# 320 unused bytes ahead of the experts' activations in SBUF

## The chip, the cores and the metric

The kernel runs on one NeuronCore of a Trainium2 chip. The metric is the device time of one execution in microseconds (us). The median of three runs of the kernel before is 1845.49 us (1844.25 to 1846.53). The profile comes from a further execution, which took 1848.51 us, 1846.7 us of it between the first and the last instruction.

## The reference

One layer: a gated short convolution, then a mixture of 16 SwiGLU experts in which each expert chooses its 256 tokens out of 2048. The model width and the experts' inner width are both 1024, and everything is float32.

```python
hl = modulate(rms_norm(lat, norm_g[i, 0]), sh1, sc1)
gate_b, gate_c, v = jnp.split(hl @ w_in, 3, axis=-1)
lat = lat + g1 * ((gate_b * dwconv_centred(gate_c * v, conv_w)) @ w_out)
hl2 = modulate(rms_norm(lat, norm_g[i, 1]), sh2, sc2)
lat = lat + g2 * expert_choice_ffn(hl2, router, w_gate, w_up, w_down)

def expert_choice_ffn(h, w_router, w_gate, w_up, w_down):
    cap = EC_CAPACITY_FACTOR * N // N_EXPERTS            # 256
    aff = jax.nn.softmax((h @ w_router).astype(jnp.float32), axis=-1)
    g, idx = lax.top_k(jnp.swapaxes(aff, 1, 2), cap)
    xs = jax.vmap(lambda hb, ib: hb[ib])(h, idx)
    hid = silu(einsum('becd,edf->becf', xs, w_gate)) * einsum('becd,edf->becf', xs, w_up)
    ys = einsum('becf,efd->becd', hid, w_down) * g[..., None]
    return zeros.at[idx].add(ys)                         # by token
```

## The kernel before

Every large product is made of three matmuls in the type float32r, on a high part and a low part of each operand: high times high, high times low, low times high. ScalarE (ACT) copies a float32 tile into its high part, and VectorE (DVE) subtracts that from the original to get the low part. Such a group of three is called a triple below.

**The mixer stages.** The input projection (L514, L515, L517), its recombined form (L875 to L877) and the output projection (L1133, L1134, L1136) multiply tiles from the pool `mix` with split weights `ws` from the pool `weights`, or two tiles of `mix` with each other. Their matmuls stream 512 columns.

**The experts.** A piece of weights (512 KB) is loaded by SyncE's queue into `raw`, split into one of eight buffers `ws`, and used from there. `gate_up(e, fh)` makes one half of an expert's inner activations. Its stationary operand is a 128x128 block of `ws`, its moving operand 256 columns of the gathered tokens `xT` (L1604, L1606, L1608), 192 matmuls in all. Then SiLU and the product go through `sg`, and the split result lands in `hT`, of which there are four buffers (L1614 to L1619). `down(e, dh)` multiplies the other way round: the stationary operand is a 128x128 block of `hT`, the moving operand 512 columns of `ws` (L1671 to L1673). It makes 48 matmuls, 16 triples, and the scaled result goes to `ot` (L1690), from which GpSimd's queue scatters it into the output. The second half of the last expert (`last_down`) makes 8 triples of that kind and then 48 matmuls of 256 columns (L1660 to L1662).

The order of the work is written out by hand: for expert e from 2 on, `gate_up(e, 0)`, `down(e-1, 0)`, `gate_up(e, 1)`, `down(e-1, 1)`. `pick` (L1534), which makes the list of an expert's tokens with 16 small bf16 matmuls, stands inside `down(e-1, 0)`, ahead of its third k. For the third expert, it stands inside `gate_up(1, 1)`.

**Where tiles lie.** A pool lays its tiles one behind the other in each partition, in the order in which their tags are first asked for. In the pool `moe`, that order is `raw`, `ax`, `oh`, `xs`, `xT`, `hT`, `sg`, `ot`. The byte address of a tile within its partition, modulo 512, is called its remainder here. All offsets that a matmul adds inside these tiles are multiples of 512 bytes, so an operand has the remainder of its tile. In the built program:

| tile | first address | remainder before | remainder of the change |
|---|---|---|---|
| `ws`, eight buffers (weights) | 44928 | 384 | 384 |
| matmul operands of the mixer (`hl`, `sb`, `tg`) | 130432 | 384 | 384 |
| `xT`, two buffers | 147008 | 64 | 64 |
| `hT`, four buffers | 179776 | 64 | 384 |
| `sg`, two buffers | 212544 | 64 | 384 |
| `ot`, three buffers | 216640 | 64 | 384 |

The other tiles of the pool stand ahead of `hT` and keep their addresses.

Of the kernel before, what the change touches and what calls it, by code (L numbers as in the profile page):

```python
# [7 lines left out]
F32 = mybir.dt.float32  # L8
# [9 lines left out]
P = 128  # L18
# [28 lines left out]
def block_kernel(ctx: ExitStack, tc, x, c, ada_w, ada_b, norm_g, w_in, conv, w_out, router, wg, wu, wd, out):  # L47
# [188 lines left out]
    def split_high(i):  # L236
        nonlocal n_high
        while n_high <= min(i, len(pieces) - 1):
            load_to(n_high)
            t = wpool.tile([P, 2] + pieces[n_high][3], F32R, name="ws", tag="ws", bufs=n_split)  # L240
            nc.scalar.activation(t[:, 0], raws[n_high], AF.Copy)  # L241
            ws_of[n_high] = t
            n_high += 1

    def split_low(i, eng=None, part=0, n=1):
        nonlocal n_done
        split_high(i)
        t, raw = ws_of[i], raws[i]
        w = pieces[i][3][-1] // n
        s = slice(part * w, (part + 1) * w)  # L250
        (eng or nc.vector).tensor_sub(t[:, 1, ..., s], raw[..., s], t[:, 0, ..., s].bitcast(F32))  # L251
        if part == n - 1:
            raws.pop(i)
            if i in extra:
                extra.remove(i)
            n_done += 1
            load_to(i + depth())
# [1255 lines left out]
    moe = ctx.enter_context(tc.tile_pool(name="moe", bufs=1, reuse_waits="tile"))  # L1513
# [72 lines left out]
    def gate_up(e, fh, between=lambda k: None):  # L1586
        xT = xT_of[e]
        if fh == 0:
            hT_of[e] = {}
        ps = [[mm.tile([P, 2, CAP], F32, name="pm", tag="mm") for _ in range(2)] for _ in range(2)]  # L1590
        for kk in range(KD // 2):
            for j in range(2):
                k = 2 * kk + j
                n = w_moe[0, e, fh, kk] + n_split - 2 + j
                split_high(n)
                between(k)
                while n_done <= min(n, len(pieces) - 1):
                    split_low(n_done)
                for f in range(4):
                    c0 = slice(f * P, (f + 1) * P)  # L1600
                    for m in range(2):
                        o = ps[m][f // 2][:, f % 2]
                        w = ws_of[w_moe[m, e, fh, kk]]
                        nc.tensor.matmul(o, w[:, 0, j, c0], xT[:, 0, k], start=(k == 0 and f % 2 == 0), stop=False,  # L1604
                                         skip_group_check=True)
                        nc.tensor.matmul(o, w[:, 0, j, c0], xT[:, 1, k], start=False, stop=False,  # L1606
                                         skip_group_check=True)
                        nc.tensor.matmul(o, w[:, 1, j, c0], xT[:, 0, k], start=False, stop=(k == KD - 1),  # L1608
                                         skip_group_check=True)
        hT = moe.tile([P, 2, 4, CAP], F32R, name="hT", tag="hT", bufs=4)  # L1610
        hT_of[e][fh] = hT
        sgs = [moe.tile([P, 2, CAP], F32, name="sg", tag="sg", bufs=2) for _ in range(2)]
        for f2, sg in enumerate(sgs):
            nc.scalar.activation(sg, ps[0][f2], AF.Silu)  # L1614
            nc.vector.tensor_mul(sg, sg, ps[1][f2])
        for f2, sg in enumerate(sgs):
            t = slice(2 * f2, 2 * f2 + 2)
            nc.scalar.activation(hT[:, 0, t], sg, AF.Copy)
            nc.vector.tensor_sub(hT[:, 1, t], sg, hT[:, 0, t].bitcast(F32))  # L1619
# [114 lines left out]
    for e in range(E):  # L1734
        if e == 0:
            gate_up(0, 0, lambda k: pick_oh(1) if k == 1 else pick(1) if k == 3 else
                    (tick(k), turn(1, 0) if k == 7 else None) if k in (2, 4, 5, 6, 7) else None)
            gate_up(0, 1, lambda k: join(1, k // 2 - 2) if k in (4, 6) else
                    turn(1, 1) if k == 1 else tick(k) if k in (0, 2, 3, 5) else None)
            continue  # L1740
        if e == 1:
            gate_up(1, 0, lambda k: tick(k) if k not in (0, 2) else None)
            down(0, 0, tick)
            for _ in rounds:
                pass
            pick_oh(2)
            gate_up(1, 1, lambda k: pick(2) if k == 1 else turn(2, k - 4) if k in (4, 5) else
                    join(2, 0) if k == 7 else None)
        else:
            if e + 1 < E:  # L1750
                pick_oh(e + 1)
            gate_up(e, 0)
            down(e - 1, 0, (lambda kk: pick(e + 1) if kk == 1 else None) if e + 1 < E else (lambda kk: None))
            gate_up(e, 1, (lambda k: turn(e + 1, k // 2 - 1) if k in (2, 4) else join(e + 1, 0) if k == 7 else None)
                    if e + 1 < E else (lambda k: None))
        down(e - 1, 1, (lambda kk: join(e + 1, 1) if kk == 1 else None) if e + 1 < E else (lambda kk: None))
# [24 lines left out]
```

## Time and profile before

| what | value |
|---|---|
| runs, us | 1845.49, 1844.25, 1846.53 |
| profiled execution, us | 1848.51 |
| its span, us | 1846.7 |
| mean granted TensorE clock | 0.988 |
| VectorE, ScalarE, GpSimd busy | 69%, 50%, 17% |
| the experts' matmuls, first to last start | 766.5 to 1836.9 us |

Starts and durations are of one profiled execution. The recorded duration of a matmul (276 ns with 256 columns, about 390 ns with 512) is longer than the time from its start to the next one's, since matmuls overlap in the array. The time that a stream of matmuls takes is therefore read from the distance of their starts, not from their durations. A start is given to 0.01 us by the timeline, so a distance is taken over many matmuls.

### The profile page before, as it was taken

To read this page: it belongs to the slowest core of one execution; us is meant where nothing else is said; L and a number is where in the kernel's file an instruction comes from. 1 tells how busy PE (TensorE), PEld (TensorE's weight loads), DVE (VectorE), ACT (ScalarE), POOL (GpSimd) and SP (SyncE) were. 2 spreads that over 40 slices of the span, in tenths; PEclk is the share of its full clock that TensorE was granted. 3 is DMA by queue.
4 is the path that set the end of the run, shared out by engine and by line. 5 is a ranking of instruction groups with operands and counts; after the bars stand their busy time and mean duration, and the time that the engine had idled before them with its cause. 6 is when DMAs were issued, how large, how long until landed. Compare 5 with 4: busy or idle time off the path is not lost.

```text
span 1846.7 us, 29333 instructions
## 1 busy us (share of the span) xinstructions
PE 1791.2 (97%) x11415; PEld 1594.1 (86%) x11415; DVE 1281.7 (69%) x1840; ACT 919.6 (50%) x1244; POOL 320.2 (17%) x466
## 2 busy tenths in 40 slices
PE   7999999999999997699999999999999999999997
PEld 6787888788888885698899999999999999999996
DVE  6787878888766678786765666666576566666653
ACT  4665454333345555474554455455455445545541
POOL 2324101111111223200210210211121021021002
PEclk9999999999999998799999999999999999999999
DMA  9756566555578994677687787877978878787774
GB/s 338 238 178 205 168 224 192 169 170 152 169 241 258 242 258 153 204 224 206 216 240 242 250 231 230 256 224 236 256 223 244 240 250 232 230 257 226 233 223 80
DMA packets 309771, 406.78 MB, mean 220 GB/s; under 512 B 103284, under 2 KB 174240, under 8 KB 309632
## 3 DMA queue, kind: packets, MB, share of 16 engines
q1 hardware_dynamic: 283632, 312.59, 55.7%
q0 software_dynamic: 26000, 92.33, 16.8%
q8 instruction: 89, 1.46, 0.3%
q14 instruction: 50, 0.41, 0.1%
HBM read 318.34 MB, written 63.98 MB: 207 GB/s over the span
## 4 chain that ended last, share of the span: by engine, by line
PE 88%; DVE 5%; DMA 2%; ACT 2%; issue 1%; POOL 0%; SPq 0%; POOLq 0%; DVEq 0%; ACTq 0%
PE pm L1604 12%; PE pm L1606 12%; PE pm L1608 12%; PE pm L876 7%; PE pm L877 7%; PE pm L875 7%; PE pm L1673 6%; PE pm L1671 6%; PE pm L1672 6%; PE pm L1133 2%; PE pm L1134 2%; PE pm L1136 2%; PE pm L514 1%; PE pm L515 1%; PE pm L517 1%
## 5 line engine op out<-in xcount | busy, mean ns | idle before, releaser
L251 DVE TENSOR_TENSOR ws<-raw,ws 128x1024 fp32r<-128x1024 f32 x390 | 463.8, 1222 | 272.9 <-ACT ws L241 272.9
L241 ACT ACTIVATE ws<-raw 128x1024 fp32r<-128x1024 f32 x390 | 394.5, 1053 | 408.8 <-PE pm L1608 325.2
L1604 PE MATMUL pm<-xT,ws 128*128 128x256 f32 x2048 | 568.6, 278 | 1.1 <-ACT xT L1583 1.1
L1606 PE MATMUL pm<-xT,ws 128*128 128x256 f32 x2048 | 567.3, 277 | 1.9 <-DVE xT L1584 1.8
L1608 PE MATMUL pm<-xT,ws 128*128 128x256 f32 x2048 | 566.9, 277 | 0.0
L1606 PEld LDWEIGHTS pm<-xT,ws 128*128 128x128 f32 x2048 | 385.9, 188 | 3.9 <-DVE xT L1584 2.1
L1604 PEld LDWEIGHTS pm<-xT,ws 128*128 128x128 f32 x2048 | 385.2, 188 | 2.7 <-ACT xT L1583 1.5
L1608 PEld LDWEIGHTS pm<-xT,ws 128*128 128x128 f32 x2048 | 385.2, 188 | 0.0
L1701 POOL DMA_INDIRECT out_dram<-ot,idx x30 | 105.0, 3498 | 587.9 <-DVE ot L1690 583.9
L1673 PE MATMUL pm<-ws,hT 128*128 128x512 f32 x504 | 198.4, 394 | 0.0
L1671 PE MATMUL pm<-ws,hT 128*128 128x512 f32 x504 | 198.3, 393 | 0.0
L1672 PE MATMUL pm<-ws,hT 128*128 128x512 f32 x504 | 197.1, 391 | 0.0
L875 PE MATMUL pm<-tg,sb 128*128 128x512 f32 x472 | 185.8, 394 | 0.0
L877 PE MATMUL pm<-tg,sb 128*128 128x512 f32 x472 | 183.8, 389 | 0.0
L876 PE MATMUL pm<-tg,sb 128*128 128x512 f32 x472 | 183.6, 389 | 0.0
L855 DVE TENSOR_TENSOR sb<-raw,sb 128x512 fp32r<-128x512 f32 x144 | 99.0, 690 | 66.3 <-ACT sb L854 65.8
L1673 PEld LDWEIGHTS pm<-ws,hT 128*128 128x128 f32 x504 | 94.7, 188 | 20.1
L1672 PEld LDWEIGHTS pm<-ws,hT 128*128 128x128 f32 x504 | 94.7, 188 | 19.9
L1671 PEld LDWEIGHTS pm<-ws,hT 128*128 128x128 f32 x504 | 94.7, 188 | 18.7
L854 ACT ACTIVATE sb<-raw 128x512 fp32r<-128x512 f32 x144 | 88.4, 625 | 39.6 <-DVE raw L861 18.2
L876 PEld LDWEIGHTS pm<-tg,sb 128*128 128x128 f32 x472 | 88.6, 188 | 19.2 <-issue 1.0
L875 PEld LDWEIGHTS pm<-tg,sb 128*128 128x128 f32 x472 | 88.6, 188 | 19.2 <-issue 1.0
(385 smaller groups left out, 2617.0 us busy)
## 6 DMA issues: line engine op xcount, KB each, us to landing
raw<-in_moe_w_down_dram SPq DMA_DIRECT2D x128, 512.0 KB, 4.8
raw<-in_moe_w_gate_dram SPq DMA_DIRECT2D x126, 512.0 KB, 4.9
raw<-in_moe_w_up_dram SPq DMA_DIRECT2D x126, 512.0 KB, 4.2
raw<-in_sc_w_in_dram SPq DMA_DIRECT2D x42, 512.0 KB, 3.9
xt<-in_x_dram SPq DMA_DIRECT2D x32, 512.0 KB, 6.8
aw<-in_ada_w_dram POOLq DMA_DIRECT2D x32, 512.0 KB, 4.3
fu<-fscr SPq DMA_DIRECT2D x23, 512.0 KB, 4.7
hl<-in_ada_w_dram SPq DMA_DIRECT2D x32, 256.0 KB, 6.3
```

Source lines behind the costliest of these rows:

```text
L241: nc.scalar.activation(t[:, 0], raws[n_high], AF.Copy)
L251: (eng or nc.vector).tensor_sub(t[:, 1, ..., s], raw[..., s], t[:, 0, ..., s].bitcast(F32))
L875: nc.tensor.matmul(o, t[:, 0, j], r[:, 0], start=(first and j == 0), stop=False, skip_group_check=True)
L876: nc.tensor.matmul(o, t[:, 1, j], r[:, 0], start=False, stop=False, skip_group_check=True)
L877: nc.tensor.matmul(o, t[:, 0, j], r[:, 1], start=False, stop=end, skip_group_check=True)
L1604: nc.tensor.matmul(o, w[:, 0, j, c0], xT[:, 0, k], start=(k == 0 and f % 2 == 0), stop=False, skip_group_check=True)
L1606: nc.tensor.matmul(o, w[:, 0, j, c0], xT[:, 1, k], start=False, stop=False, skip_group_check=True)
L1608: nc.tensor.matmul(o, w[:, 1, j, c0], xT[:, 0, k], start=False, stop=(k == KD - 1), skip_group_check=True)
L1671: nc.tensor.matmul(ps[s], h, w[:, 0, j], start=(k == 0), stop=False)
L1672: nc.tensor.matmul(ps[s], h, w[:, 1, j], start=False, stop=False)
L1673: nc.tensor.matmul(ps[s], l, w[:, 0, j], start=False, stop=(k == KD - 1))
L1701: st = nc.gpsimd.indirect_dma_start(out=out_rows, out_offset=bass.IndirectOffsetOnAxis(ap=idx_of[e][:, s:s + 1], axis=0), in_=ots[s], in_o ...
```

## The change

One tile of 80 float32 (320 bytes per partition) is asked for from the pool `moe`, once, just ahead of the first `hT`. Nothing reads or writes it. `hT`, `sg` and `ot` move up by 320 bytes, and nothing else moves.

```diff
@@ gate_up
                         nc.tensor.matmul(o, w[:, 1, j, c0], xT[:, 0, k], start=False, stop=(k == KD - 1),
                                          skip_group_check=True)
+        if (e, fh) == (0, 0):
+            moe.tile([P, 80], F32, name="gap", tag="gap", bufs=1)
         hT = moe.tile([P, 2, 4, CAP], F32R, name="hT", tag="hT", bufs=4)
         hT_of[e][fh] = hT
```

The built program has the same instructions in the same order on every engine, with the same waits, shapes and operands. Only the addresses of `hT`, `sg` and `ot` differ.

## The prediction

> **What bounds the kernel now.** I read the page's shares first, then the chain that ended last, then the waits of the elementwise engines, and last the starts of single matmuls.
>
> ```profile
> span 1846.7 us, 29333 instructions
> PE 1791.2 (97%) x11415; PEld 1594.1 (86%) x11415; DVE 1281.7 (69%) x1840; ACT 919.6 (50%) x1244; POOL 320.2 (17%) x466
> PE 88%; DVE 5%; DMA 2%; ACT 2%; issue 1%; POOL 0%; SPq 0%; POOLq 0%; DVEq 0%; ACTq 0%
> L251 DVE TENSOR_TENSOR ws<-raw,ws 128x1024 fp32r<-128x1024 f32 x390 | 463.8, 1222 | 272.9 <-ACT ws L241 272.9
> L241 ACT ACTIVATE ws<-raw 128x1024 fp32r<-128x1024 f32 x390 | 394.5, 1053 | 408.8 <-PE pm L1608 325.2
> ```
>
> TensorE is busy for 97% of the span and makes 88% of the chain. The split of the weights, the largest work of ScalarE, waits 325.2 us for the gate/up matmuls (L1608), and VectorE's part waits for ScalarE. So in the experts the elementwise engines follow TensorE, and the time there is the number of matmuls by the distance of their starts. The change adds and moves no instruction. It can act on the time only through what a different address does to a read or a write, and on the end only where it alters the distance of matmul starts.
>
> **Three distances.** First the mixer, where both operands have remainder 384: a window of 80 us, and single starts of one triple.
>
> ```profile
> 250.00:330.00 80.00, 80.00 (x354) 66.25 (x353) 68.21 (x96) 44.84 (x71) 6.08 (x11) 1.00 0.64 204
> 340.21 0.39 PE L875 MATMUL pm<-tg,sb 128*128 128x512 f32 x1
> ...
> 340.89 0.39 PE L875 MATMUL pm<-tg,sb 128*128 128x512 f32 x1
> ```
>
> The first bracket counts the matmuls that touch the window. With the one that is cut at its edge taken off, 353 fill 80.00 us: 226.6 ns each, at a granted clock of 1.00. The triple from 340.21 to 340.89 takes 0.68 us, which is the same.
>
> Second the experts, where `hT` (64) is loaded against `ws` (384) in `down`, and `ws` (384) against `xT` (64) in gate/up. These are the first matmul of `down(6, 1)`, the first of the gate/up half that follows, and the first behind that.
>
> ```profile
> 1276.13 0.39 PE L1671 MATMUL pm<-ws,hT 128*128 128x512 f32 x1
> ...
> 1287.12 0.28 PE L1604 MATMUL pm<-xT,ws 128*128 128x256 f32 x1
> ...
> 1308.90 0.39 PE L1671 MATMUL pm<-ws,hT 128*128 128x512 f32 x1
> ```
>
> The 48 matmuls of `down` take 10.99 us, 229.0 ns each, a triple 0.687 us. The 192 of gate/up take 21.78 us, 113.4 ns each: two of them take as long as one of the mixer's (226.9), so gate/up shows no loss although its remainders are unequal too. The lines' durations say the same of `down`, by line: minimum, median, maximum in ns.
>
> ```profile
> L1671 PE MATMUL pm<-ws,hT x504: 388/388/482, 837.0 to 1830.9; 128*128 128x512 f32 x168
> L1672 PE MATMUL pm<-ws,hT x504: 387/392/398, 837.3 to 1831.1; 128*128 128x512 f32 x168
> L1673 PE MATMUL pm<-ws,hT x504: 388/394/398, 837.5 to 1831.3; 128*128 128x512 f32 x168
> L876 PE MATMUL pm<-tg,sb x472: 387/389/396, 103.9 to 520.3; 128*128 128x512 f32 x158
> L877 PE MATMUL pm<-tg,sb x472: 388/389/398, 104.1 to 520.5; 128*128 128x512 f32 x158
> ```
>
> In the mixer the medians are 389 and 389. In `down` they are 388, 392 and 394. Three times 389 is 1167, the three of `down` make 1174: 7 ns a triple, as the starts say (687 against 680).
>
> Third, there is a stretch in which both expert stages are spaced wider still, from one `pick` (854.73) to the next (915.30).
>
> ```profile
> 854.73 0.26 PE L1534 MATMUL pi<-ax,oh 128*128 128x10 bf16 x4 [0.34 <-DVE oh L1526]
> 854.84 0.36 PE L1604 MATMUL pm<-xT,ws 128*128 128x256 f32 x1
> ...
> 874.71 0.40 PE L1671 MATMUL pm<-ws,hT 128*128 128x512 f32 x1
> ...
> 885.68 0.39 PE L1673 MATMUL pm<-ws,hT 128*128 128x512 f32 x1
> ...
> 915.30 0.56 PE L1534 MATMUL pi<-ax,oh 128*128 128x10 bf16 x16
> ```
>
> There 168 gate/up matmuls take 19.87 us, 118.3 ns with the first (about 0.09 us long) and 117.8 without it, and the first 47 of `down` take 10.97 us, 233.4 ns. So the spacing takes more than one value with the same addresses, and the matmuls of a `pick` can switch it.
>
> **The change, part by part.** (1) `hT` moves from 64 to 384. In `down` both operands then have the remainder that the mixer's have. Forecast: the distance becomes the mixer's. 504 triples by 0.687 - 0.680 = 0.007 us are 3.5 us. That is the largest value of this term. The smallest is nothing, if the remainder isn't what holds the 229. The value taken is the upper end, because the nearest stream to `down`, the output projection, has `ws` as its moving operand too, in another order of operands than L875's, and reaches the same distance.
>
> (2) A settling loss. After a break, the distance isn't reached at once. These rows are the output projection behind the router's small matmuls.
>
> ```profile
> 624.86 0.39 PE L1134 MATMUL pm<-ws,hl 128*128 128x512 f32 x1
> ...
> 626.93 0.62 PE L1136 MATMUL pm<-ws,hl 128*128 128x512 f32 x2
> 627.38 0.39 PE L1133 MATMUL pm<-ws,hl 128*128 128x512 f32 x1
> ...
> 634.18 0.39 PE L1133 MATMUL pm<-ws,hl 128*128 128x512 f32 x1
> ```
>
> From 627.38 to 634.18 it makes 30 matmuls, six for each of five k: 226.7 ns each, as (1) says. Between the first two starts lie nine distances in 2.07 us. Nine of 226.7 ns are 2.04, so a break costs 0.03 us. The halves of `down` have 32 entries, and 13 of them have a `pick` inside: at most 45 by 0.03 = 1.4 us. I take half, 0.7, since an entry from gate/up is a change of shape without a pause and the mixer shows no row for that. Bounds: 0 to 1.4.
>
> (3) `sg` and `ot` move too. Their writers and readers are ACT, DVE and the scatter.
>
> ```profile
> L1619 DVE TENSOR_TENSOR hT<-sg,hT 128x512 fp32r<-128x512 f32 x64 | 42.8, 689 | 3.2
> L855 DVE TENSOR_TENSOR sb<-raw,sb 128x512 fp32r<-128x512 f32 x144 | 99.0, 690 | 66.3 <-ACT sb L854 65.8
> L1618 ACT ACTIVATE hT<-sg 128x512 fp32r<-128x512 f32 x64 | 39.9, 631 | 26.3 <-DVE sg L1615 26.3
> L854 ACT ACTIVATE sb<-raw 128x512 fp32r<-128x512 f32 x144 | 88.4, 625 | 39.6 <-DVE raw L861 18.2
> ```
>
> DVE's subtraction of 128x512 takes 689 ns at remainder 64 and 690 at 384, ACT's copy 631 and 625. The difference is at most 64 by 6 ns = 0.4 us on an engine that waits for TensorE anyway: nothing. If that cover were gone, 0.4 us. The scatter from `ot` has no reader in the kernel that TensorE waits for; nothing.
>
> Sum: 3.5 - 0.7 = **2.8 us less**. The profiled execution would take 1848.51 - 2.8 = 1845.7 us. The runs' median lies 3.0 us below it, and on that scale the forecast is 1845.5 - 2.8 = **1842.7 us**.
>
> A rule that speaks against the change stands in the Trainium skill, SBUF — State Buffer, section "Who interferes with whom": TensorE has two independent read ports, one for the moving operand and one for the weights, and never waits on anyone. By it an address changes nothing, and the sum is 0: 1845.5 us. The trace bears it out only in part, since 226.6, 229.0 and 233.4 ns stand for one shape at one clock. The page TensorE: Matmul & The Clock Gate, section "Back-to-back issue gap", gives N / 2.4 + 2.5, which is 216 ns for 512 columns (estimate by that page), and no stage here reaches it.
>
> **The rivals.** *The remainder is not the cause.* Gate/up speaks for it: its remainders are unequal and it loses nothing. So does the wide stretch, in which the distance changes with no address changed. The mixer's two orders of operands, both at 226.7, speak against it. The distance stays at 229: 1845.5 us, with the runs' own spread of about 1 us to either side.
>
> *More goes than `down`'s loss.* The wide stretch follows a `pick`, and the phase in which the matmuls meet it depends on what ran before, which the change alters. If the stretch runs at the usual distances, 168 and 192 gate/up matmuls save 4.4 ns each, 1.6 us, and 60 matmuls of `down` up to 4.4 ns, 0.3 us. With the 2.8: 1845.5 - 4.7 = 1840.8 us. The chance of it is even at best, and the stretch may also stay.
>
> *The wide spacing is caught more often.* Place: the `pick` inside each `down(e-1, 0)`, from 915.30 on. Price: from one `pick` to the next, 384 gate/up matmuls by 117.8 - 113.4 = 4.4 ns and 96 of `down` by about 4.4 ns are 2.1 us an expert. It decides from the second expert caught on, which uses up the 2.8. The experts repeat the same code, so one in three of 13 may be caught (8.4 us: 1851 us) or all (27 us: 1870 us). For it: this spacing exists and lasted four stages. Against it: after 915.30 no further stretch of it, so that the usual spacing is the rule behind a `pick`.
>
> **How the numbers follow.** Forecast, the distance becomes the mixer's: 0.52. Remainder not the cause: 0.15. More goes: 0.17. Wide spacing caught: 0.16. A measurement of this kernel can tell about 0.2%, 3.7 us, from no change; that bound is 1841.8 us. The forecast's own gain runs from 2.1 (3.5 - 1.4) to 3.5, and with the runs' spread about a third of it passes the bound. Faster by over 0.2%: 0.17 + a third of 0.52 = 0.34. Slower by over 0.2%: the wide spacing, and a little of the rest: 0.17. Within 0.2%: 0.49. The range takes in the forecast, the third case with a microsecond of spread below it, and the unchanged time with as much above it: 1839.5 to 1847.0 us. It leaves out the wide spacing.
>
> **What would show it.** Right: the 48 matmuls of a `down` half take 10.88 to 10.92 us, the three lines' medians become 389, and gate/up keeps 21.78. Step (1) is wrong if a half still takes 10.99. Step (2) is wrong if a half takes over 10.95 with its last triples at 0.680. The wide spacing would show as gate/up halves of 22.6 us. What would make the whole wrong is a distance set by something that neither stage shows, such as the phase in which `down` takes over from gate/up. `hT` could then settle at a third value, above 229.

## The result, and the profile after

The changed kernel takes 1866.11 us (median of four runs, 1865.94 to 1867.59) against 1844.87 us before: the ratio is 1.0116, with a 95% interval from 1.0103 to 1.0128. It is 21 us slower, outside the range. The profiled execution's span grew from 1846.7 to 1865.8 us. These are the page's lines that answer to the ones shown of before.

```profile
span 1865.8 us, 29333 instructions
PE 1810.2 (97%) x11415; PEld 1615.9 (87%) x11415; DVE 1281.4 (69%) x1840; ACT 919.1 (49%) x1244; POOL 320.5 (17%) x466
PE 86%; DVE 5%; DMA 4%; ACT 2%; issue 2%; POOL 0%; SPq 0%; POOLq 0%; DVEq 0%; ACTq 0%
L251 DVE TENSOR_TENSOR ws<-raw,ws 128x1024 fp32r<-128x1024 f32 x390 | 463.5, 1221 | 289.1 <-ACT ws L241 289.1
L241 ACT ACTIVATE ws<-raw 128x1024 fp32r<-128x1024 f32 x390 | 394.2, 1051 | 425.5 <-PE pm L1608 340.7
```

TensorE's busy time grew by 19.0 us, as the span did by 19.1, with the same number of matmuls. The elementwise engines' busy times are the same, and they wait longer for gate/up (340.7 us, before 325.2). So the time went into the distances of the matmuls. Gate/up halves at 113.4 ns are called narrow below, those at 117.8 wide. In the changed kernel the lines of `down` are L1673 to L1675. This is one line each of the source view, as shown of before.

```profile
L1673 PE MATMUL pm<-ws,hT x504: 387/389/482, 837.3 to 1849.5; 128*128 128x512 f32 x168
L1674 PE MATMUL pm<-ws,hT x504: 387/389/397, 837.6 to 1849.7; 128*128 128x512 f32 x168
L1675 PE MATMUL pm<-ws,hT x504: 388/389/397, 837.8 to 1849.9; 128*128 128x512 f32 x168
```

The medians are 389, 389, 389, as in the mixer. And here are the timeline's rows of `down(6, 1)`, of the gate/up half behind it, and of the first matmul that follows.

```profile
1283.33 0.39 PE L1673 MATMUL pm<-ws,hT 128*128 128x512 f32 x1
...
1294.21 0.28 PE L1604 MATMUL pm<-xT,ws 128*128 128x256 f32 x1
...
1316.82 0.39 PE L1673 MATMUL pm<-ws,hT 128*128 128x512 f32 x1
```

`down` takes 10.88 us (before 10.99): 226.7 ns a matmul. Gate/up takes 22.61 us (before 21.78): 117.8 ns instead of 113.4. The windows view of one whole expert, two gate/up and two `down` halves, shows the balance, with before first and the changed kernel second (its columns are those of the 80 us window above).

```profile
1155.00:1221.06 66.06, 66.06 (x497) 61.91 (x496) 42.87 (x50) 33.25 (x37) 10.47 (x5) 1.00 0.80 239
```

```profile
1159.17:1226.71 67.54, 67.54 (x498) 63.56 (x496) 42.85 (x50) 33.24 (x36) 10.47 (x5) 1.00 0.79 234
```

An expert takes 1.48 us more: 2 x 0.83 for gate/up, less 0.18 for `down`. Thirteen such experts are 19.2 us, about the growth of the span. It isn't all that changed: from the start of `gate_up(2, 1)` to that of the last `down` half the growth is 19.8 us (880.0 to 899.8), and the first experts ahead of it took 0.9 us less, mainly because `gate_up(2, 0)` was wide before and narrow here.

The gate/up halves are wide from their first matmuls on. These are the entries after `down(1, 1)`, before and in the changed kernel.

```profile
956.82 0.28 PE L1604 MATMUL pm<-xT,ws 128*128 128x256 f32 x1
956.94 0.28 PE L1606 MATMUL pm<-xT,ws 128*128 128x256 f32 x1
957.05 0.28 PE L1608 MATMUL pm<-xT,ws 128*128 128x256 f32 x1
...
957.53 0.28 PE L1604 MATMUL pm<-xT,ws 128*128 128x256 f32 x1
957.64 0.28 PE L1606 MATMUL pm<-xT,ws 128*128 128x256 f32 x1
957.75 0.28 PE L1608 MATMUL pm<-xT,ws 128*128 128x256 f32 x1
```

```profile
956.63 0.28 PE L1604 MATMUL pm<-xT,ws 128*128 128x256 f32 x1
956.75 0.28 PE L1606 MATMUL pm<-xT,ws 128*128 128x256 f32 x1
956.87 0.28 PE L1608 MATMUL pm<-xT,ws 128*128 128x256 f32 x1
956.98 0.28 PE L1604 MATMUL pm<-xT,ws 128*128 128x256 f32 x1
...
957.34 0.28 PE L1604 MATMUL pm<-xT,ws 128*128 128x256 f32 x1
...
957.69 0.28 PE L1604 MATMUL pm<-xT,ws 128*128 128x256 f32 x1
```

Before, the first six distances add up to 0.71 us (118 each), then they drop to 0.11. In the changed kernel they stay where they start (0.36 and 0.35 us for the next two triples). Neither `xT` nor `ws` has moved between the two.

The weights' loads show the two distances as well. In the narrow half of before from 1287.12, the median load takes 188 ns in all three lines. In the wide half of the changed kernel from 1294.21, it takes 192 ns in L1608 and 188 in the other two, and in the wide stretch of before (856 to 874 us) 192 in L1606 alone. Whether the longer load is the cause or a sign of the spacing, no run shows.

The last half of the last expert shows a second loss. Its 48 matmuls of 256 columns on `hT` (from 1831.57 before, from 1850.17 in the changed kernel) start 113.3 ns apart before and 120.0 in the changed kernel, where both operands have remainder 384. That is 0.3 us, and a first sign that equal remainders don't suit short matmuls.

### The profile page after: what moved, and what is told of

Read it like the earlier page. It is cut to its first block, busy times and chain, and to the rows that moved or that the text cites. A ratio compares the mean times of both kernels' runs of the same rounds, so it can differ in the third digit from the quotient of the medians.

```text
span 1865.8 us, 29333 instructions
## 1 busy us (share of the span) xinstructions
PE 1810.2 (97%) x11415; PEld 1615.9 (87%) x11415; DVE 1281.4 (69%) x1840; ACT 919.1 (49%) x1244; POOL 320.5 (17%) x466
## 4 chain that ended last, share of the span: by engine, by line
PE 86%; DVE 5%; DMA 4%; ACT 2%; issue 2%; POOL 0%; SPq 0%; POOLq 0%; DVEq 0%; ACTq 0%
PE pm L1604 12%; PE pm L1606 12%; PE pm L1608 12%; PE pm L876 7%; PE pm L875 7%; PE pm L877 7%; PE pm L1673 6%; PE pm L1675 6%; PE pm L1674 6%; DMA hl<-hl 2%; PE pm L1133 1%; PE pm L1134 1%; PE pm L1136 1%; PE pm L514 1%; PE pm L515 1%
## 5 line engine op out<-in xcount | busy, mean ns | idle before, releaser
L241 ACT ACTIVATE ws<-raw 128x1024 fp32r<-128x1024 f32 x390 | 394.2, 1051 | 425.5 <-PE pm L1608 340.7
L1604 PE MATMUL pm<-xT,ws 128*128 128x256 f32 x2048 | 576.8, 282 | 1.0 <-ACT xT L1583 1.0
L1606 PE MATMUL pm<-xT,ws 128*128 128x256 f32 x2048 | 575.6, 281 | 1.9 <-DVE xT L1584 1.8
L1608 PE MATMUL pm<-xT,ws 128*128 128x256 f32 x2048 | 575.2, 281 | 0.0
L1608 PEld LDWEIGHTS pm<-xT,ws 128*128 128x128 f32 x2048 | 392.9, 192 | 0.0
L1606 PEld LDWEIGHTS pm<-xT,ws 128*128 128x128 f32 x2048 | 385.3, 188 | 3.7 <-DVE xT L1584 2.1
L1673 PE MATMUL pm<-ws,hT 128*128 128x512 f32 x504 | 197.8, 392 | 0.0
L1675 PE MATMUL pm<-ws,hT 128*128 128x512 f32 x504 | 196.3, 389 | 0.0
L1675 PEld LDWEIGHTS pm<-ws,hT 128*128 128x128 f32 x504 | 94.6, 188 | 20.0
L1673 PEld LDWEIGHTS pm<-ws,hT 128*128 128x128 f32 x504 | 94.6, 188 | 17.9
L875 PEld LDWEIGHTS pm<-tg,sb 128*128 128x128 f32 x472 | 88.6, 188 | 19.2 <-issue 1.0
```

Of the source, the lines that this page charges most:

```text
L875: nc.tensor.matmul(o, t[:, 0, j], r[:, 0], start=(first and j == 0), stop=False, skip_group_check=True)
L1673: nc.tensor.matmul(ps[s], h, w[:, 0, j], start=(k == 0), stop=False)
L1675: nc.tensor.matmul(ps[s], l, w[:, 0, j], start=False, stop=(k == KD - 1))
```

## The experiments

Two theories were open. H: at gate/up's addresses there are two steady distances, and the way in which it is entered from `down` chooses. R: gate/up is wide because the other tiles have left remainder 64. Times are medians in us; e2, e4 to e14 and e17 were timed once, in the profiled execution. "Before" is the kernel before on the same chip, timed beside the run.

**e1: the pad ahead of `xT`.**

```diff
         if i == 0:
+            moe.tile([P, 80], F32, name="gap", tag="gap", bufs=1)
             xT_of[e] = moe.tile([P, 2, KD, CAP], F32R, name="xT", tag="xT", bufs=2)
...
-        if (e, fh) == (0, 0):
-            moe.tile([P, 80], F32, name="gap", tag="gap", bufs=1)
```

> The pad stands ahead of the tokens xT instead of hT, so xT, hT, sg and ot all have remainder 384, as the split weights. Theory H (handover: at unequal remainders gate/up has two steady distances, 113.3 and 117.8 ns, and takes the wide one when it is entered without a break from down at 226.7 ns): with equal remainders gate/up has, as the mixer, one distance only, so all 27 uninterrupted gate/up halves take 21.8 us, the down halves 10.88 us, and the kernel about 1845 - 3 to 5 = 1840 to 1842 us. Rival R (static: gate/up is wide because hT, sg and ot have left remainder 64, whatever comes ahead of it): gate/up stays at 22.6 us a half, 1866 us.

1880.88 us, ratio 1.0204 (1.0187 to 1.0221): slower than the changed kernel, which no theory had. A gate/up half and the start behind it:

```profile
1299.49 0.28 PE L1605 MATMUL pm<-xT,ws 128*128 128x256 f32 x1
...
1322.53 0.40 PE L1672 MATMUL pm<-ws,hT 128*128 128x512 f32 x1
```

The half takes 23.04 us, 120.0 ns a matmul, alike in all halves. So equal remainders are best for 512 columns and bad for 256: there is one distance, as H said, but a long one. If a matmul's time is a fixed part plus a part in proportion to its columns, and both are the same for the two shapes at equal remainders, then 256 columns cost 226.7 - 120.0 = 106.7 ns and the fixed part is 13.3 ns. This is an estimate, and two shapes alone can't test it.

**e2: `sg` and `ot` alone.** The pad stands between `hT` and `sg`.

```diff
         hT_of[e][fh] = hT
+        if (e, fh) == (0, 0):
+            moe.tile([P, 80], F32, name="gap", tag="gap", bufs=1)
         sgs = [moe.tile([P, 2, CAP], F32, name="sg", tag="sg", bufs=2) for _ in range(2)]
```

> The pad stands behind hT, so sg and ot alone move to remainder 384 and hT stays at 64. Theory H: sg and ot are no operands of a matmul, so down stays at 229 ns (10.99 us a half), gate/up at 113.4 (21.78 us a half), and the time is that of the kernel before, 1845 us within 2. Rival R, if it comes by ACT's, DVE's or the scatter's use of sg and ot: gate/up halves of 22.6 us, 1866 us.

1841.41 us, before 1844.58. The later halves take 10.99 and 21.78 us, as before. R falls for `sg` and `ot`: it is `hT` that counts.

**e3: a break at the entry of gate/up.** The changed kernel with one small matmul ahead of a half's first one.

```diff
+                if k == 0 and (e > 1 or (e, fh) == (1, 1)):
+                    brk = tp.tile([P, 4], F32, name="brk", tag="tp")
+                    nc.tensor.matmul(brk, same, cnts[0], start=True, stop=True)
                 for f in range(4):
```

> The changed kernel with one added matmul of 4 columns (its result is read by nobody) at the start of each gate/up half from the second half of the second expert on, 29 in all, each some 0.09 us. Theory H: the handover is broken, gate/up goes to 113.4 ns, 21.8 to 21.9 us a half with the break, down stays at 226.7: 1866 + 29 x 0.09 - 27 x 0.83 = 1846 us. Rival R: gate/up stays at 117.8 and the breaks only add, 1866 + 2.6 = 1869 us.

1846.36 us, ratio 1.0008 (0.9996 to 1.0020). All 27 later halves are narrow, with every address as in the changed kernel. The entry after `down(6, 1)`:

```profile
1285.09 0.17 PE L1601 MATMUL brk<-cnt,same 128*128 128x4 f32 x1
1285.12 0.36 PE L1607 MATMUL pm<-xT,ws 128*128 128x256 f32 x1
1285.32 0.28 PE L1609 MATMUL pm<-xT,ws 128*128 128x256 f32 x1
...
1306.98 0.39 PE L1676 MATMUL pm<-ws,hT 128*128 128x512 f32 x1
```

The first distance takes 0.20 us, some 0.09 more than a usual one, and the half 21.86. The loss goes with nothing but 29 small matmuls: 27 halves get 0.75 us back, 20 us. R falls altogether: the addresses alone don't make gate/up wide.

**e4 to e8 and e10 to e12: other remainders.** The same pad with another size (64, 192, 128, 32 and 256 bytes for e4 to e7 and e10), or one ahead of `xT` (32 bytes for e8), or two (128 and 192 bytes ahead of `xT` and `hT` for e11, 192 and 128 for e12).

> A pad of 64 bytes instead of 320: hT, sg and ot at remainder 128, unequal to the weights' 384 but, as 384, a multiple of 128. Theory H with the remainder difference as the cause: down keeps a distance above 226.7 (as at 64) and hands over well, gate/up 113.4, about 1845 us. A variant, that alignment to 128 bytes and not equality makes down's 226.7: down at 226.7 and gate/up at 117.8, 1866 us.

> hT, sg and ot at remainder 256. The run with 128 gave down 226.7 ns and gate/up 117.8, so equality modulo 512 isn't needed. 128 and 384 are still equal modulo 256; 256 and 384 are equal modulo 128 alone. Theory A (what counts is the remainder difference modulo 128): down 226.7, gate/up halves 22.6 us, 1866 us within 4. Rival (modulo 256): down keeps about 229 as at 64, gate/up 21.8, 1845 us.

> hT, sg and ot at remainder 192, which differs from the weights' by 64 modulo 128, as 64 does. Theory A: down 229 ns, 10.99 us a half, gate/up 21.8 us a half, 1845 us within 4. Rival (only the exact remainder 64 keeps gate/up at 113.3, any other is as 128 and 384): gate/up halves of 22.6 us, 1866 us.

> hT, sg and ot at remainder 96, a difference of 96 modulo 128 that no run has had. Theory A says only that down has one of the known distances or a new one between 220 and 234; by theory H gate/up follows from it: 113.3 if down's distance isn't 226.7, 117.8 if it is. Rival to H (gate/up wide whenever hT isn't at a difference of 64): gate/up halves of 22.6 us whatever down shows.

> A pad of 32 bytes ahead of xT: xT, hT, sg and ot all at 96. With xT at 384 gate/up took 120.0 ns everywhere, with 64 it takes 113.3 or 117.8. Theory A (each load of weights costs a sum that the difference modulo 128 sets: 13.3 ns at 0, less at 64 with 256 columns): a difference of 96 gives a third value for gate/up, between 107 (256 columns at the mixer's 512-column rate less the 13.3 ns) and 120, alike in all uninterrupted halves. Rival (two classes only, multiples of 128 and all others): gate/up 113.3 or 117.8 as before.

> hT, sg and ot at remainder 320. Theory A fell with 256 (down 230 to 233 ns) and 192 (233 ns). Theory B: the distance goes by the remainder difference modulo 256, as 128 and 384 gave the same 226.7. 320 equals 64 modulo 256: down 228.9 ns, 10.99 us a half, gate/up 113.3 in all later halves, 21.8 us, the kernel before's time, 1845 us within 3. Rival (modulo 512): something else, down above 229 or gate/up at 117.8, over 1852 us.

> xT at remainder 192, hT, sg and ot at 384. Theory B: down 226.7 as at 384 before. Gate/up is at a difference of 192 modulo 256 (weights less xT), which down has in the kernel before and no gate/up run has had; so far it was 113.3 or 117.8 at 64, 118.3 at 32, 120.0 at 0. If the number of columns doesn't matter for what a load of weights costs beside the stream, as 120.0 - 106.7 = 226.7 - 213.3 = 13.3 ns at 0 suggests, then the lowest is 228.9 - 106.7 = 122.2 ns; if unequal remainders help the short matmuls, 113.3 to 118.

> xT at remainder 256, hT, sg and ot at 384: a difference of 128 modulo 256 for gate/up. Theory B: down 226.7. Gate/up by the same two readings: above 120 ns if the cost of a load goes by the difference alone (down showed 230 to 233 at 128, less 106.7 is 123 to 127), or 113.3 to 118 if every inequality helps the short matmuls. Either would be one distance for all halves or two.

The table gives the remainders, the halves of `down` without a `pick`, the later gate/up halves (from the start of a half's first matmul to the first one behind it), and the time. `ws` is at 384 in all.

| run | `xT` | `hT` | `down`, us | gate/up, us | time | before |
|---|---|---|---|---|---|---|
| before | 64 | 64 | 10.99 | 21.78 | 1844.87 | |
| changed | 64 | 384 | 10.88 | 22.61 | 1866.11 | 1844.87 |
| e4 | 64 | 128 | 10.88 | 22.61 | 1863.25 | 1844.58 |
| e10 | 64 | 320 | 10.99 | 21.78 | 1846.79 | 1847.43 |
| e5 | 64 | 256 | 11.15 | 21.76 and 22.61 in turn | 1861.95 | 1846.16 |
| e6 | 64 | 192 | 11.20 | 21.78 and 22.62, two of each | 1864.14 | 1846.16 |
| e7 | 64 | 96 | 11.20 | 22.61 | 1872.69 | 1846.16 |
| e8 | 96 | 96 | 11.20 | 22.73 | 1876.75 | 1846.16 |
| e11 | 192 | 384 | 10.92 | 22.62 | 1869.52 | 1847.43 |
| e12 | 256 | 384 | 10.92 | 23.04 | 1880.46 | 1847.43 |
| e1 | 384 | 384 | 10.91 | 23.03 | 1880.88 | 1844.58 |

128 and 384 give the same halves, and so do 64 and 320. Alignment to 128 bytes, which e4 left open, fell with e5. Theory A (the difference modulo 128) fell with e5 and e6, and theory B (modulo 256) stands in both pairs. The difference here is the address of the stationary operand less that of the moving one, modulo 256. For 512 columns, equal is best: the halves of the table give 226.7 ns at 0, 228.9 at 192, 232 at 128, and 233.3 at 64 and 224. For 256 columns equal is worst: gate/up takes 120.0 ns at 0 and 128, 118.3 at 32, 117.8 at 192, and 113.4 or 117.8 at 64. The 117.8 of e11 lies in one of the two ranges that were expected, the 120.0 of e12 in neither. `ws` is at 384 in every run, so the runs don't tell the difference of two addresses from the remainder of the other tile alone.

Runs e5 and e6 also refute H as it was first put. Their `down` isn't at 226.7, yet gate/up is wide in half of its halves. In e5, what stands in the `down` half ahead goes with it: the 13 halves behind a `pick` are narrow, the 14 behind a `down` half without one are wide. In e6 that isn't enough. These are the starts of four gate/up halves in a row and of the `down` halves behind them.

```profile
1628.69 0.28 PE L1604 MATMUL pm<-xT,ws 128*128 128x256 f32 x1
...
1651.31 0.39 PE L1673 MATMUL pm<-ws,hT 128*128 128x512 f32 x1
...
1663.01 0.28 PE L1604 MATMUL pm<-xT,ws 128*128 128x256 f32 x1
...
1685.63 0.39 PE L1673 MATMUL pm<-ws,hT 128*128 128x512 f32 x1
...
1696.83 0.28 PE L1604 MATMUL pm<-xT,ws 128*128 128x256 f32 x1
...
1718.61 0.39 PE L1673 MATMUL pm<-ws,hT 128*128 128x512 f32 x1
...
1730.30 0.28 PE L1604 MATMUL pm<-xT,ws 128*128 128x256 f32 x1
...
1752.08 0.39 PE L1673 MATMUL pm<-ws,hT 128*128 128x512 f32 x1
```

The halves take 22.62, 22.62, 21.78 and 21.78 us, in one execution, with the same remainders. The second and the fourth both stand behind a `down` half with a `pick`, that is, behind the same code, and differ. Behind a `pick`, a half of e6 is as the gate/up half before it; behind a `down` half without one, it is the other way; all 26 transitions follow this. So either something is carried from half to half, or the buffers count, since `hT`'s four and `xT`'s two come round every four halves. The buffers alone don't choose: `gate_up(15, 1)` uses the same ones as `gate_up(13, 1)`, has no `pick` ahead of it, and is narrow (21.78) where the other is wide (22.62).

**e9: a break within a half.** As e3, at `k == 4` of the first halves only.

> The changed kernel with the small matmul in the middle (ahead of k = 4) of the first gate/up half of each expert from the third on, 14 in all; the second halves have none. Theory H, in the form that the runs left of it (gate/up has two steady distances at one set of addresses; the entry chooses, and it is held until a break): in those halves the 96 matmuls ahead of the break at 117.8, the 96 behind it at 113.3; the second halves, entered anew from down at 226.7, at 117.8 throughout, 22.6 us. Time 1866 - 14 x (0.42 - 0.09) = 1861 us. Rival (a break helps by what else it moves, for example the splits' phase): no change of distance at the break within a half.

1869.06 us, before 1847.43. Wide on both sides of the break:

```profile
1294.88 0.28 PE L1607 MATMUL pm<-xT,ws 128*128 128x256 f32 x1
...
1306.19 0.17 PE L1601 MATMUL brk<-cnt,same 128*128 128x4 f32 x1
1306.21 0.36 PE L1607 MATMUL pm<-xT,ws 128*128 128x256 f32 x1
1306.41 0.28 PE L1609 MATMUL pm<-xT,ws 128*128 128x256 f32 x1
...
1317.60 0.39 PE L1676 MATMUL pm<-ws,hT 128*128 128x512 f32 x1
```

96 matmuls in 11.31 us ahead of it, 95 in 11.19 behind the first one: 117.8 ns both. H's "until a break" falls too. A break is no reset.

**e13: e3's break in the kernel before.** The same three lines, without the pad.

> The kernel before (hT at 64) with the 29 small matmuls of the break run at the gate/up entries. Two readings of that run are left. Reset: a break ahead of the first matmul of a half always brings 113.3, so nothing changes here but 29 x 0.09: gate/up 21.86 us a half, 1847.5 us. Phase: the entry decides by when its first matmuls meet the weights' loads, and a break only shifts that, for better or worse; then some or all halves here may go to 117.8, up to 27 x 0.83 = 22 us more, 1870 us. The break in mid-half, which left 117.8 as it was, speaks for the second.

1871.64 us, before 1844.99. The break that mends the changed kernel spoils the kernel before. Its later halves run wide, wide, wide, narrow in turn. Two of them:

```profile
1228.43 0.36 PE L1607 MATMUL pm<-xT,ws 128*128 128x256 f32 x1
...
1251.12 0.40 PE L1674 MATMUL pm<-ws,hT 128*128 128x512 f32 x1
...
1262.72 0.36 PE L1607 MATMUL pm<-xT,ws 128*128 128x256 f32 x1
...
1284.58 0.39 PE L1674 MATMUL pm<-ws,hT 128*128 128x512 f32 x1
```

22.69 and 21.86 us. Reset falls. The reading by phase is left, as an argument: no run measures a phase. `down` loses too, at the addresses of the kernel before: its halves without a `pick` take 11.02 us (228.9 ns) behind a narrow half and 11.23 (233.3 ns) behind a wide one. So `down` also has two distances at one difference, as the wide stretch of the kernel before has it (233.4).

**e14, e16 and e17: a shift without a pause.** The changed kernel with the last matmul of a `down` half made as two of 256 columns (e17: the last two matmuls).

```diff
             nc.tensor.matmul(ps[s], h, w[:, 1, j], start=False, stop=False, skip_group_check=True)
+            if (k, s) == (KD - 1, 1) and e < E - 1:
+                for c in (slice(0, CAP), slice(CAP, H)):
+                    nc.tensor.matmul(ps[s][:, c], l, w[:, 0, j, c], start=False, stop=True, skip_group_check=True)
+                return
             nc.tensor.matmul(ps[s], l, w[:, 0, j], start=False, stop=(k == KD - 1), skip_group_check=True)
```

> The changed kernel with the last matmul of each down half of the experts 0 to 14 made as two of 256 columns, which adds one load of weights and some 13 ns a half. Phase reading: the handover is shifted without a pause, so gate/up's distance may change, to 113.3 (1866 - 22 = 1844 us) or not (1866 us). Rival, only a pause or a foreign matmul changes it: 117.8 in all halves as in the changed kernel.

> The same kernel as e14_last_split, timed. Its trace had gate/up at 113.3 ns in all later halves and down at 226.7; the distances above these add up to 1.8 us where the kernel before has 6.5 (2.6 in gate/up, 3.9 in down), and the split adds 29 x 0.013 = 0.4. Expected 1844.9 - 4.3 = 1840.6 us, ratio 0.9977, faster than before and than the changed kernel. If gate/up's distance at one entry is a matter of chance from run to run, single times of 1850 to 1866 us would show.

> The changed kernel with the last two matmuls of each down half of the experts 0 to 14 made as two of 256 columns each. Phase reading (only where the stream stands at the entry counts, in steps that a matmul of 256 columns shifts): the shift is another one than in e14_last_split, so gate/up may be at either distance, 1841 us or 1864 us, and no rule of mine says which. Rival (a matmul of 256 columns with equal remainders ahead of the entry is what brings 113.3, whatever the count): 113.3 in all later halves, 1841.5 us.

e14 took 1841.15 us (before 1844.99), e17 1847.59 (before 1843.62). All later gate/up halves are narrow in all three traces, and `down` is at 226.7. The handover of e14 after `down(6, 1)`:

```profile
1280.64 0.40 PE L1677 MATMUL pm<-ws,hT 128*128 128x256 f32 x2
1280.87 0.29 PE L1604 MATMUL pm<-xT,ws 128*128 128x256 f32 x1
1280.99 0.28 PE L1606 MATMUL pm<-xT,ws 128*128 128x256 f32 x1
...
1302.65 0.39 PE L1673 MATMUL pm<-ws,hT 128*128 128x512 f32 x1
```

21.78 us. No pause is needed. Over twelve runs, e16 has a median of 1842.90 against 1843.62, ratio 0.9994 (0.9984 to 1.0004): as fast as the kernel before, not shown to be faster. The expected 4.3 us was too much. It counted losses of the first experts too, and these differ at the same operand addresses: `gate_up(2, 0)` took 25.36 us before and 23.03 in e2. In the later ones, e16 takes 65.91 us an expert (1147.97 to 1213.88) against 66.06, which is 2.0 us for thirteen, within the interval. e17, with two split matmuls, is narrow as e14 is. It doesn't tell a shift from the mere presence of a short matmul of equal remainders.

**e15: the kernel before with all of `down` in matmuls of 256 columns.**

```diff
-            nc.tensor.matmul(ps[s], h, w[:, 0, j], start=(k == 0), stop=False)
-            nc.tensor.matmul(ps[s], h, w[:, 1, j], start=False, stop=False)
-            nc.tensor.matmul(ps[s], l, w[:, 0, j], start=False, stop=(k == KD - 1))
+            for c in (slice(0, CAP), slice(CAP, H)):
+                o, first = ps[s][:, c], k == 0 and c.start == 0
+                nc.tensor.matmul(o, h, w[:, 0, j, c], start=first, stop=False, skip_group_check=True)
+                nc.tensor.matmul(o, h, w[:, 1, j, c], start=False, stop=False, skip_group_check=True)
+                nc.tensor.matmul(o, l, w[:, 0, j, c], start=False, stop=(k == KD - 1), skip_group_check=True)
```

> The kernel before with every down triple made as two triples of 256 columns, as the last down of the kernel before does in its second part, where they were 113.3 to 114 ns apart. At that, a half of down takes 96 x 113.3 = 10.88 us instead of 10.99, 32 halves save 3.5 us, and gate/up comes from a stream of its own distance: if it stays at 113.3, 1841 to 1842 us, ratio 0.998. If the short matmuls of down take the wide distance (117.8), 11.3 us a half, 10 us more; if gate/up takes it too, 32 us more.

1858.59 us, ratio 1.0069 (1.0053 to 1.0086). Both stages are wide in every other half: gate/up takes 22.62 and 21.77 us in turn, and the `down` halves behind them have medians of 118 ns (11.81 us, a `pick` among them) and 113 ns (10.88 us). `down`, now a stream of gate/up's own shape, keeps the distance that gate/up hands it. Gate/up doesn't keep `down`'s: all 26 later halves behind these take the other one. The last of them, `gate_up(15, 1)`, has no `pick` ahead of it and is narrow behind a wide `down`, so the `pick` isn't what turns it here.

## Why the prediction was wrong

Step (1) was right in cause and size. `down` went from 229.0 to 226.7 ns, its three medians became 389, and a half takes 10.88 us. The 504 triples saved what was forecast, and e4 and e10 show that the remainder does it, though modulo 256 and not 512.

Step (2), the settling of `down`, was too large. A half without a `pick` takes 10.88 us = 48 x 226.7 ns, with nothing lost at the entry. One with a `pick` takes 11.39 or 11.43 us, 0.08 to 0.12 less than before, so at most 0.03 us is lost there.

Step (3) was right: e2 shows that `sg` and `ot` cost nothing.

The step that failed is one that the sum didn't have. The prediction read "gate/up shows no loss although its remainders are unequal too" from one half, and let it stay at 21.78 us, since none of its operands moved. But the wide stretch of the same trace had shown gate/up at 117.8 ns with those operands. It was weighed as a rival, at 0.16, with its place at the `pick`. Its place is the handover from `down` to gate/up, and 27 later halves pay 0.83 us each, 22.4 us. That is the rival's case of all experts caught (it named 1870 us), with a price of 1.66 us an expert instead of 2.1, because `down` itself isn't wide. Its sign, gate/up halves of 22.6 us, came true, and its place didn't, so the nearness of 1870 to 1866 is in part luck. The prediction also named the handover as what would make the whole wrong, but the one into `down`, and there the forecast held. The runs show that the handover chooses (e3 and e14 undo the loss with the addresses unchanged), that both distances occur in one execution with one set of remainders (e5, e6, e13), and that the narrow halves of the kernel before were no property of gate/up's own addresses (e13 loses most of them).

From the rule in the Trainium skill, SBUF — State Buffer, section "Who interferes with whom", that TensorE never waits on anyone, the prediction drew that an address changes nothing. The runs don't agree: `down` takes 226.7 ns with `hT` at 384 and 228.9 with it at 64, and e2 shows that the two tiles that moved with it don't matter.

What stays open is the rule by which an entry leads to one distance or the other. Neither the distance of `down` (e6 has both behind 233.3 ns, e13 both behind 228.9), nor the `pick` ahead (e5 and e15 differ), nor a break as such (e3 against e9 and e13) decides it alone. That it is a matter of phase between the stream and the weights' loads is an argument: the phase wasn't measured, and what other engines read and write at that time wasn't varied by itself.

## What to carry to other kernels

Where a stage is a dense stream of matmuls, a change of an address can change its rate and that of the stage behind it: measure the distance of starts in every stage that follows, not only in the stage whose operand moved. If one trace shows a stage at two rates, then the better one is not guaranteed, and an edit upstream may lose it; price that rate for all of the stage before taking a gain of a few nanoseconds elsewhere. Here the loss could be mended with the tiles left where they are, by splitting the last matmul ahead of the stage (e16), which gave the time of the kernel before and no shown gain.

## What the runs showed of the hardware

- The distance of float32r matmuls, each with its own load of weights, goes with the address of an operand modulo 256 bytes. With the difference taken as above: 512 columns start 226.7 ns apart at 0 (the changed kernel), 228.9 or 233.3 at 192 (both in e13), 232 at 128 (e5), and 233.3 at 64 and 224 (e6, e7). 256 columns start 120.0 ns apart at 0 (e1, and on `hT` in the last half of the changed kernel) and at 128 (e12), 118.3 at 32 (e8), and 113.3 or 117.8 at 64 (e6) and at 192 (both in e15).
- Equal addresses modulo 256 are best for 512 columns and worst for 256.
- An estimate from 226.7 and 120.0 ns: 106.7 ns for 256 columns and a fixed 13.3 ns at equal addresses. By it the fixed part is 6.7 ns for a narrow gate/up matmul (113.3 - 106.7) and 20.0 for 512 columns at the worst (233.3 - 213.3).
- At one difference, a stream can have two steady distances, each for hundreds of matmuls at a granted clock of 1.00 (113.3 and 117.8 ns for gate/up). Which one is taken goes with what ran ahead: e5 alternates by halves, e6 and e13 repeat every four, and the changed kernel has 27 wide ones.
- At 113.3 ns, the loads of weights take 188 ns in the median; at 117.8 ns those of one line in three take 192 (the changed kernel from 1294.21, e6 from 1663.01), and at 120.0 ns all do (e1).
